# First weights and rows in a written order, first scale spread by TensorE, and the keys of the third dilation laid side by side

## Chip, cores and metric

The kernel runs on one core of a Trainium2 chip. The metric is the time of one execution in device microseconds, as the median of several runs. The engines are TensorE (PE; its weight loads are shown as PEld), VectorE (DVE), ScalarE (ACT), GpSimd (POOL) and SyncE (SP), which here only issues transfers.

## What is computed

One layer of a decoder block on x of 2048 rows and 1024 columns, in float32, cut to what matters here:

```python
h = rmsnorm(x, norm_pre_mix)
proj = h @ w_in                                  # 1024 x 5376
q, k = rope(proj[..., Q0:K0]), rope(proj[..., K0:V0])   # 12 heads of 64
v = proj[..., V0:U0]
# three groups of four heads: dilation 1, 4, 16; each residue class is a causal
# band over 128-query blocks
y_attn = softmax-merge of the three groups
y_gmlp = gelu(u) * spatial(layernorm(gelu(z)))
x = x + rmsnorm((gate_a * (y_attn @ w_a) + gate_b * (y_gmlp @ w_b)) @ w_out, norm_post_mix)
x = x + rmsnorm(relu(rmsnorm(x, norm_pre_mlp) @ w_mlp_in) ** 2 @ w_mlp_out, norm_post_mlp)
```

With dilation 16 a sequence of 2048 has 16 residue classes of 128 positions each, so one block of queries sees one block of keys.

## The kernel before

Rows go in four chunks `c` of 512, each of four blocks `i` of 128. Matrix products run as three matmuls (`mm3`, lines 95 to 97): every operand is split into a rounded high half (fp32r) and the rest, the low half, and high times high, high times low and low times high are added up in PSUM. `split` (lines 70 to 78) makes the halves: a copy for the high one on ScalarE or POOL, a subtraction for the low one on VectorE or POOL.

The program is written in a framework that places the semaphores. TensorE's instructions run in the order in which they are written (line 56). On the other engines and on SP's queue a scheduler orders them by the place in the text and by what is ready in its own model of the times, except where a block is put under `as_written()` (the order of the text on ScalarE, VectorE, POOL and SP) or under `behind()` (each instruction is queued behind the last one so far on its engine, with no wait for its end). Before the change both are used only in the MLP, from line 1143 on.

The start: the scale `norm_pre_mix` is broadcast to 128 partitions by a transfer of 512 KB on ScalarE's queue (`gpre`, line 330). Six fp32 matmuls on a tile of ones (`busy`, line 339) run while the first rows come. The loads of the first rows, of the identity and of the three first weights (`raws`, each in two halves, g = 0, 1, 2) are queued on SP. `prenorm_rows` squares the rows of a block, makes the reciprocal root (`rstd_of`) and multiplies rows, rstd and scale on VectorE (line 192). `prenorm_cols` transposes the block on TensorE (line 202), splits the transposes into `hT` (lines 205 and 206) and, for the first two chunks, copies them once more and stores them (lines 209 and 210). `v_block` then projects a block to the values: for block (0,0) group 0, group 1, the transposes of block (0,1), group 2; for the later ones both wide groups in one, with the transposes of the next block after half of the steps. The split of the first weights is dealt out to POOL, ScalarE and VectorE by `early_split`.

Then `qk_pair` makes queries and keys (`which` 0 and 1) of the three dilations. VectorE multiplies by cosine and sine into `t1` and `t2`, POOL adds or subtracts into `r` with the columns in the order of the dilation (lines 287, 289, 293), ScalarE and VectorE split `r`, and the result is stored in `qk_d`.

Attention runs in 48 units of one dilation `g`, one chunk or residue class `c`, one head `j`, four blocks `b` each, with projection steps (`steps`) between its parts on TensorE. `attn_load` brings `kp` and `qq`; for g = 2 `kp` holds the queries and `qq` the keys. The scores of the third dilation are the four matmuls at line 580, with `kp` as the stationary and `qq` as the moving side; those of the others are at lines 583 and 584. Line 580's operands are `kp[:, b:512:4]` and `qq[:, :, b::4]`: in the stored order the four residues of a class group lie next to each other, and a block takes every fourth element. After the units `combine` merges the three dilations; its transposes are at line 689.

Of the kernel before, what the change touches and what calls it, by code (L numbers as in the profile page):

```python
# [27 lines left out]
def f32(ap):  # L28
    return ap.bitcast(F32) if ap.dtype != F32 else ap
# [12 lines left out]
def block_kernel(ctx, tc, a, out):  # L42
# [120 lines left out]
    sm = stack(e1, "sm", 2)  # L163
    st = stack(e1, "st", 2)

    hT = {}
    xts = {}

# [8 lines left out]
            sp.dma_start(xt[:, sl], x[c * 512 + i * P:c * 512 + (i + 1) * P, sl])  # L177
        xts[c, i] = xt

    def prenorm_rows(c, i):  # L180

        if (c, i) not in xts:
            load_x(c, i)
        xt = xts[c, i]
        ss = sm.tile([P, 2], F32, name=f"ss_{c}{i}", tag="ss")
        for hf in range(2):
            junk = psum_aux(f"junk_{c}{i}{hf}")
            act.activation(junk, xt[:, hf * 512:(hf + 1) * 512], AF.Square, accum_out=ss[:, hf:hf + 1])
        dve.tensor_add(ss[:, 0:1], ss[:, 0:1], ss[:, 1:2])
        r = rstd_of(sm, ss[:, 0:1], 1, 1.0 / D, f"pre{c}{i}")  # L190
        for sl in cuts(c, i):
            dve.scalar_tensor_tensor(xt[:, sl], xt[:, sl], r, gpre[:, sl], op0=OP.mult, op1=OP.mult)

    def prenorm_cols(c, i):

        if i == 0:
            hT[c] = hp.tile([P, 2, KT, 512], F32R, name=f"hT_a{c}", tag="hT", bufs=2)
        h, xt = hT[c], xts.pop((c, i))
        for k in range(0, KT, 4):
            pt = psum_aux(f"pt_{c}{i}{k}")  # L200
            for kk in range(4):
                pe.transpose(pt[:, kk * P:(kk + 1) * P], xt[:, (k + kk) * P:(k + kk + 1) * P], ident)
            hh, hl = (h[:, o, k:k + 4, i * P:(i + 1) * P] for o in range(2))
            p3 = pt.rearrange("p (k t) -> p k t", k=4)
            act.activation(hh, p3, AF.Copy)
            dve.tensor_sub(hl, p3, f32(hh))
            if c < 2:
                raw = xp.tile([P, 4, P], F32, name=f"hr_{c}{i}{k}", tag="hr", bufs=3)
                act.activation(raw, p3, AF.Copy)
                sp.dma_start(hT_d[c, :, k:k + 4, i * P:(i + 1) * P], raw)  # L210
# [55 lines left out]
    def qk_pair(rp, w, g, which, c, rope, between=None):  # L266
        d = DIL[g]
        dst = qk_d[g][which]
        nm = f"{g}{which}{c}"
        pp = []  # L270
        for m in range(2):
            p = psum_mm(f"x{m}_{nm}")
            for n, _ in enumerate(steps_T(w, m, c, p)):
                if between and n in (3, 7):
                    between(m * 2 + n // 4)
            pp.append(p)
        p1, p2 = pp
        cs, sn = rope[:, 0, :], rope[:, 1, :]
        hl = rp.tile([P, 4, 512], F32R, name=f"hl_{nm}", tag="hl", bufs=2)
        for o, (pa, pb, op) in enumerate(((p1, p2, OP.subtract), (p2, p1, OP.add))):  # L280
            t1 = rp.tile([P, 512], F32, name=f"t1_{nm}{o}", tag="t1", bufs=2)
            t2 = rp.tile([P, 512], F32, name=f"t2_{nm}{o}", tag="t2", bufs=2)
            dve.tensor_mul(t1, pa, cs)
            dve.tensor_mul(t2, pb, sn)
            r = rp.tile([P, 512], F32, name=f"r_{nm}{o}", tag="r", bufs=2)
            if d == 1:
                pool.tensor_tensor(r, t1, t2, op=op)  # L287
            elif d == 4:
                pool.tensor_tensor(r.rearrange("p (r l) -> p r l", r=d),
                                   t1.rearrange("p (l r) -> p r l", r=d),  # L290
                                   t2.rearrange("p (l r) -> p r l", r=d), op=op)
            else:
                pool.tensor_tensor(r.rearrange("p (m l r) -> p m l r", m=4, r=4),
                                   t1.rearrange("p (l m r) -> p m l r", m=4, r=4),
                                   t2.rearrange("p (l m r) -> p m l r", m=4, r=4), op=op)
# [31 lines left out]
    with ExitStack() as e1a:  # L327
        xp = stack(e1a, "xp", 2)
        gpre = xp.tile([P, D], F32, name="gpre", bufs=1)
        act.dma_start(gpre, bcast(a["norm_pre_mix"]))  # L330
        act.activation(warm, eps, AF.Sqrt)
        rp = stack(e1a, "rp", 1, side="right")

        busy = rp.tile([P, 256], F32, name="busy", tag="t1", bufs=2)
        dve.memset(busy, 1.0)
        for n in range(2):
            p = psum_aux(f"busy{n}")
            for _ in range(3):
                pe.matmul(p[:, :256], busy[:, :P], busy, start=True, stop=True)
        load_x(0, 0)  # L340
        sp.dma_start(ident, a["ident"])
        raws = [rp.tile([P, 2, 4, 256], F32, name=f"raw{g}", tag=t, bufs=2) for g, t in enumerate(("hl", "hl", "vt"))]
        wide0 = wide_tiles("wv0")
        third0 = wp.tile([P, 2, 2, 4, 256], F32R, name="wv02", tag="w", bufs=3)
# [3 lines left out]
            for kk in range(2):  # L348
                sp.dma_start(raws[g][:, kk], w_src(6 + g, kk))

        def early_split(g, *engs):
            for kk in range(2):
                w = part(wide0[kk], g) if g < 2 else third0[:, kk]
                split(w[:, 0], w[:, 1], raws[g][:, kk], *engs[kk])

        early_load(0)
        load_x(0, 1)
        early_load(1)
        early_load(2)
        prenorm_rows(0, 0)  # L360
        early_split(0, ("pool", "dve"), ("act", "dve"))
        prenorm_cols(0, 0)
        prenorm_rows(0, 1)
        early_split(1, ("act", "pool"), ("act", "dve"))
        early_split(2, ("act", "dve"), ("pool", "dve"))
        blocks = [(c, i) for c in range(4) for i in range(4)]
        qk = [(g, which) for g in range(3) for which in range(2)]
        for half in range(2):
            ropes = {}
            for c in (2 * half, 2 * half + 1):  # L370
                ropes[c] = rp.tile([P, 2, 512], F32, name=f"rope{c}", tag="rope", bufs=2)
# [12 lines left out]
            for n, (g, which) in enumerate(qk):  # L384
                w = nxt
                if n + 1 < len(qk):
                    g2, w2 = qk[n + 1]
                    nxt = load_w(w2 * 3 + g2, f"wq{g2}{w2}{half}")
                elif not half:
                    wv = load_wide(6, "wv1"), load_w(8, "wv12")  # L390
                qk_pair(rp, w, g, which, 2 * half, ropes[2 * half])
                between = None
                if not half and n == 5:
                    for i in range(4):
                        prenorm_rows(2, i)
                    between = lambda i: prenorm_cols(2, i)
                qk_pair(rp, w, g, which, 2 * half + 1, ropes[2 * half + 1], between)
# [156 lines left out]
    def attn_unit(g, c, j):  # L554
# [18 lines left out]
        for b2 in range(2):  # L573
            sp_ = psum_aux(f"s_{nm}{b2}")
            for i in range(2):
# [1 line left out]
                w0, bsl = info[b][0], slice(b * P, (b + 1) * P)  # L577
                o = sp_[:, i * 256:(i + 1) * 256]
                if g == 2:
                    pe.matmul(o.rearrange("p (h k) -> p h k", h=2), kp[:, b:512:4], qq[:, :, b::4],  # L580
                              start=True, stop=True)
                else:
                    pe.matmul(o, qq[:, 0, bsl], kp[:, w0:w0 + 256], start=True, stop=False)
                    pe.matmul(o, qq[:, 1, bsl], kp[:, w0:w0 + 256], start=False, stop=True)
# [555 lines left out]
                    lone_a(1, q, n_, raw.rearrange("p (k c) -> p k c", k=4))  # L1140


    def as_written():
        t = mybir.EngineType
        return tc.manual_schedule(engines={t.Activation, t.DVE, t.Pool, t.SP})

    def behind():

        es, t = ExitStack(), mybir.EngineType
        for e in (t.Activation, t.DVE, t.Pool, t.SP):  # L1150
            es.enter_context(tc.issue_after(next(i for i in reversed(nc.cur_bb.bb.instructions) if i.engine == e)))
        return es

    first_half, second_half = 1, 0
    e2.close()
    ea, ew = ExitStack(), ExitStack()
# [548 lines left out]
```

## Time and profile before

| | us |
|---|---|
| median of 3 runs (2775.97, 2776.09, 2780.45) | 2776.09 |
| the profiled execution | 2779.44 |
| its span | 2777.7 |
| mean granted clock of TensorE, share of full | 0.991 |
| busy: PE / DVE / ACT / POOL | 2712.0 / 1545.2 / 1051.9 / 947.3 |

Times in the trace count from the start of the span. A row of a timeline has start, length, engine, line and operation, output<-inputs, shapes and count; in brackets stands how long the engine had been idle before it and what released it. A row with a count over 1 merges that many instructions.

### The profile page before, as it was taken

What the parts mean: (1) busy time and instruction counts of PE and PEld (TensorE: products, weight loads), DVE (VectorE), ACT (ScalarE), POOL (GpSimd) and SP (SyncE); (2) the same over time, 40 slices, a digit from 0 to 9 for tenths busy, and PEclk for the clock granted to TensorE, in tenths of its full rate; (3) what the DMA queues carried; (4) which work ended last, traced back from release to release, by engine and by line L of the source; (5) the groups of instructions that cost most, each with busy time, mean ns of one, the idle gap of its engine ahead of it and who ended that gap; (6) DMA issues with size and microseconds to landing.
All of it is one profiled execution on the core that took longest, in us unless ns stands there. A gap on an engine that the chain in (4) does not pass through costs nothing. (4 is left out here: it accounts for less than half of the span.)

```text
span 2777.7 us, 34732 instructions
## 1 busy us (share of the span) xinstructions
PE 2712.0 (98%) x12668; PEld 2242.3 (81%) x12668; DVE 1545.2 (56%) x2643; ACT 1051.9 (38%) x2151; POOL 947.3 (34%) x777
## 2 busy tenths in 40 slices
PE   9999999999999999999999999999999999999998
PEld 7888888888878887787787788878887887777787
DVE  5655552344453344554556644555436777777766
ACT  5213111244453321354444544555444333233334
POOL 0341341200000013312215432223314766677645
PEclk9999999999999999999999999999999999999999
DMA  7445455466666654655658534554343122222236
GB/s 266 168 145 169 156 152 195 126 190 195 193 217 192 190 166 149 186 190 160 183 171 268 168 103 125 181 168 126 106 146 108 54 84 84 84 84 84 84 106 213
DMA packets 298380, 426.00 MB, mean 153 GB/s; under 512 B 18528, under 2 KB 172384, under 8 KB 298208
## 3 DMA queue, kind: packets, MB, share of 16 engines
q1 hardware_dynamic: 210368, 372.12, 42.3%
q10 hardware_dynamic: 87840, 51.65, 6.2%
q8 instruction: 100, 1.64, 0.2%
q14 instruction: 72, 0.59, 0.1%
HBM read 282.99 MB, written 140.71 MB: 153 GB/s over the span
## 5 line engine op out<-in xcount | busy, mean ns | idle before, releaser
L1556 PE MATMUL ya<-T_spots,s 128*128 128x512 f32 x1272 | 313.1, 392 | 4.8 <-DVE acc L1564 2.7
L1556 PEld LDWEIGHTS ya<-T_spots,s 128*128 128x128 f32 x1272 | 239.0, 188 | 59.0 <-issue 4.5
L70 ACT ACTIVATE s<-sraw 128x768 fp32r<-128x768 f32 (+1 forms) x184 | 126.0, 695 | 358.2 <-POOL sraw L1355 199.0
L1016 PE MATMUL aa<-B,A 128*128 128x512 f32 x768 | 187.0, 396 | 6.3 <-ACT xs L1030 5.1
L78 DVE TENSOR_TENSOR s<-sraw,s 128x512 fp32r<-128x512 f32 x171 | 163.6, 979 | 34.6 <-ACT s L70 33.0
L987 POOL TENSOR_TENSOR s<-w1r 128x512 f32<-128x512 f32 x32 | 43.5, 1359 | 397.3 <-DVE S L78 337.3
L1016 PEld LDWEIGHTS aa<-B,A 128*128 128x128 f32 x768 | 145.5, 190 | 40.5 <-ACT xs L1030 6.0
L72 POOL TENSOR_SCALAR w_g<-w_g_r 128x1024 fp32r<-128x1024 f32 x32 | 34.1, 1082 | 412.3 <-PE g L97 313.7
L1556 PE MATMUL yc<-T_spots,s 128*128 128x512 f32 x624 | 164.1, 394 | 3.6 <-POOL T_spots L78 3.6
L95 PE MATMUL x<-hT_a,wq 128*128 128x512 f32 x384 | 149.7, 390 | 0.0
L97 PE MATMUL x<-hT_a,wq 128*128 128x512 f32 x384 | 149.4, 389 | 0.0
L96 PE MATMUL x<-hT_a,wq 128*128 128x512 f32 x384 | 149.4, 389 | 0.0
L1556 PEld LDWEIGHTS yc<-T_spots,s 128*128 128x128 f32 x624 | 115.8, 188 | 33.6 <-POOL T_spots L78 9.7
L653 DVE TENSOR_REDUCE o<-po 128x256 f32<-128x512 f32 x48 | 33.1, 690 | 187.5 <-PE po L652 187.5
L78 POOL TENSOR_TENSOR T_spots<-w2r,T_spots 128x512 fp32r<-128x512 f32 x86 | 123.2, 1459 | 5.4 <-ACT T_spots L70 5.4
L70 ACT ACTIVATE hl<-r 128x512 fp32r<-128x512 f32 x48 | 30.4, 633 | 233.2 <-POOL r L287 89.0
L95 PE MATMUL g<-hT_b,w_g 128*128 128x512 f32 x256 | 105.0, 410 | 0.0
L95 PE MATMUL g<-hT_a,w_g 128*128 128x512 f32 x256 | 104.8, 409 | 0.0
L95 PE MATMUL o<-wo,mg 128*128 128x512 f32 x256 | 100.8, 394 | 4.1 <-ACT mg L70 4.1
L70 ACT ACTIVATE S<-w1r 128x512 fp32r<-128x512 f32 x96 | 60.0, 629 | 112.0 <-PE ac L1016 66.6
L815 POOL TENSOR_TENSOR g<-g,g 128x512 f32<-128x512 f32 x28 | 38.8, 1385 | 185.9 <-DVE g L813 179.2
L1354 POOL TENSOR_TENSOR sraw<-sraw 128x256 f32<-128x256 f32 x56 | 41.3, 737 | 174.6 <-DVE s L78 160.3
(379 smaller groups left out, 7214.4 us busy)
## 6 DMA issues: line engine op xcount, KB each, us to landing
w1r<-in_w_mlp_in_dram SPq DMA_DIRECT2D x64, 512.0 KB, 3.6
sraw<-sd SPq DMA_DIRECT2D x128, 256.0 KB, 3.4
qk<-hl SPq DMA_DIRECT2D x24, 1024.0 KB, 5.4
qq<-qk SPq DMA_DIRECT2D x96, 256.0 KB, 5.1
w_g_r<-in_w_in_dram SPq DMA_DIRECT2D x32, 512.0 KB, 5.3
gated<-gt SPq DMA_DIRECT2D x64, 256.0 KB, 3.4
g<-gated SPq DMA_DIRECT2D x64, 256.0 KB, 4.4
w2r<-in_w_mlp_out_dram SPq DMA_DIRECT2D x16, 1024.0 KB, 6.0
```

The costliest lines, as they stand in the source:

```text
L70: act.activation(hi, src, AF.Copy)
L72: pool.tensor_scalar(hi, src, 1.0, 1.0, op0=OP.mult, op1=OP.mult)
L78: (pool if lo_eng == "pool" else dve).tensor_sub(lo, src, f32(hi))
L95: pe.matmul(ps, lh, rh, start=start, stop=False)
L96: pe.matmul(ps, lh, rl, start=False, stop=False)
L97: pe.matmul(ps, ll, rh, start=False, stop=stop)
L653: dve.tensor_reduce(ot[:, :, j * 64:(j + 1) * 64], po.rearrange("p (b h e) -> p b e h", b=4, h=2), axis=AX.X, op=OP.add)
L815: (dve if dt == KT - 1 else pool).tensor_add(parts[0], parts[0], parts[1])
L987: pool.tensor_add(s1, a21, a22)
L1016: pe.matmul(p, w[:, l, k, :], h[:, r, k, :], start=i in (1, 6, 5) and not k and not n, stop=k == 3 and n == 2, skip_group_check=True)
L1354: pool.tensor_add(a22, a21, a22)
L1556: pe.matmul(p, s[:, l], w[:, r], start=i in (1, 2, 5) and not m and not o, stop=m == 1 and o == 2, skip_group_check=True)
```

## The change

1. The scale is loaded as one row of 4 KB into a zeroed tile and spread to all partitions by two fp32 matmuls with a tile of ones (`gp`, in PSUM). The first rows are multiplied from there; ScalarE copies `gp` to `gpre` later, for the rows that follow. The identity is loaded on ScalarE's queue instead of SP's.
2. Five filling matmuls stand ahead of the spread, and two behind it.
3. The loads, the preparation of block (0,0) and of the rows of (0,1), and the split of the first weights stand in a block under `as_written()`, with the shares of the engines dealt out anew. The copies and stores of the transposes of (0,0) (`keep_cols`) go to its end. What is traced from there to the end of `v_block` of (0,1) is queued `behind()` it; that includes the load of the rows of (0,2).
4. In the third dilation the keys (not the queries) are written with the rows of one residue side by side in runs of 32, by POOL's addition, and line 580 reads its moving side in these runs.

`as_written` and `behind` only move up in the text. The diff, with that move left out:

```diff
-    def prenorm_rows(c, i):
+    def prenorm_rows(c, i, gs=None):
...
-        for sl in cuts(c, i):
-            dve.scalar_tensor_tensor(xt[:, sl], xt[:, sl], r, gpre[:, sl], op0=OP.mult, op1=OP.mult)
+        for n, sl in enumerate(cuts(c, i)):
+            dve.scalar_tensor_tensor(xt[:, sl], xt[:, sl], r, gs[n] if gs else gpre[:, sl], op0=OP.mult, op1=OP.mult)
...
     def prenorm_cols(c, i):
...
+        kept = []
         for k in range(0, KT, 4):
...
             dve.tensor_sub(hl, p3, f32(hh))
+            kept.append((k, p3))
+            if (c, i) != (0, 0):
+                keep_cols(c, i, kept)
+        return kept
+
+    def keep_cols(c, i, kept):
+        while kept:
+            k, p3 = kept.pop(0)
             if c < 2:
                 raw = xp.tile([P, 4, P], F32, name=f"hr_{c}{i}{k}", tag="hr", bufs=3)
                 act.activation(raw, p3, AF.Copy)
...
-                pool.tensor_tensor(r.rearrange("p (m l r) -> p m l r", m=4, r=4),
-                                   t1.rearrange("p (l m r) -> p m l r", m=4, r=4),
-                                   t2.rearrange("p (l m r) -> p m l r", m=4, r=4), op=op)
+                order = "l r" if not which else "r l"
+                pool.tensor_tensor(r.rearrange(f"p (m {order}) -> p m {order}", m=4, r=4),
+                                   t1.rearrange(f"p (l m r) -> p m {order}", m=4, r=4),
+                                   t2.rearrange(f"p (l m r) -> p m {order}", m=4, r=4), op=op)
...
-        act.dma_start(gpre, bcast(a["norm_pre_mix"]))
+        rp = stack(e1a, "rp", 1, side="right")
+
+        row = rp.tile([P, D], F32, name="row", tag="rope", bufs=2)
+        busy = rp.tile([P, 256], F32, name="busy", tag="t1", bufs=2)
+        pool.memset(row, 0.0)
+        dve.memset(busy, 1.0)
         act.activation(warm, eps, AF.Sqrt)
-        rp = stack(e1a, "rp", 1, side="right")
-
-        busy = rp.tile([P, 256], F32, name="busy", tag="t1", bufs=2)
-        dve.memset(busy, 1.0)
+        act.dma_start(row[0:1], a["norm_pre_mix"])
+        act.dma_start(ident, a["ident"])
+        p = psum_aux("busy")
+        for _ in range(5):
+            pe.matmul(p[:, :256], busy[:, :P], busy, start=True, stop=True)
+        gp = [psum_mm(f"gpre{n}") for n in range(2)]
         for n in range(2):
-            p = psum_aux(f"busy{n}")
-            for _ in range(3):
-                pe.matmul(p[:, :256], busy[:, :P], busy, start=True, stop=True)
+            pe.matmul(gp[n], busy[:, :P], row[:, n * 512:(n + 1) * 512], start=True, stop=True)
         load_x(0, 0)
-        sp.dma_start(ident, a["ident"])
...
-        def early_split(g, *engs):
-            for kk in range(2):
-                w = part(wide0[kk], g) if g < 2 else third0[:, kk]
-                split(w[:, 0], w[:, 1], raws[g][:, kk], *engs[kk])
-
-        early_load(0)
-        load_x(0, 1)
-        early_load(1)
-        early_load(2)
-        prenorm_rows(0, 0)
-        early_split(0, ("pool", "dve"), ("act", "dve"))
-        prenorm_cols(0, 0)
-        prenorm_rows(0, 1)
-        early_split(1, ("act", "pool"), ("act", "dve"))
-        early_split(2, ("act", "dve"), ("pool", "dve"))
+        def early(g, kk):
+            w = part(wide0[kk], g) if g < 2 else third0[:, kk]
+            return w[:, 0], w[:, 1], raws[g][:, kk]
+
+        def hi(g, kk):
+            w = early(g, kk)
+            act.activation(w[0], w[2], AF.Copy)
+
+        def lo(g, kk, eng):
+            w = early(g, kk)
+            eng.tensor_sub(w[1], w[2], f32(w[0]))
+
+        with as_written():
+            early_load(0)
+            load_x(0, 1)
+            early_load(1)
+            early_load(2)
+            prenorm_rows(0, 0, gp)
+            p = psum_aux("busy")
+            for _ in range(2):
+                pe.matmul(p[:, :256], busy[:, :P], busy, start=True, stop=True)
+            hi(0, 0)
+            hi(0, 1)
+            lo(0, 0, dve)
+            kept = prenorm_cols(0, 0)
+            lo(0, 1, dve)
+            hi(1, 0)
+            hi(1, 1)
+            lo(1, 0, pool)
+            lo(1, 1, dve)
+            for n in range(2):
+                act.activation(gpre[:, n * 512:(n + 1) * 512], gp[n], AF.Copy)
+            prenorm_rows(0, 1)
+            hi(2, 0)
+            hi(2, 1)
+            lo(2, 1, pool)
+            lo(2, 0, dve)
+            keep_cols(0, 0, kept)
+        first = behind()
...
                 v_block(rp, wv, c, i, between)
+                if (c, i) == (0, 1):
+                    first.close()
...
-                    pe.matmul(o.rearrange("p (h k) -> p h k", h=2), kp[:, b:512:4], qq[:, :, b::4],
-                              start=True, stop=True)
+                    pe.matmul(o.rearrange("p (h c l) -> p h c l", h=2, c=4),
+                              kp[:, b:512:4],
+                              qq.rearrange("p h (c r l) -> p r h c l", c=4, r=4)[:, b], start=True, stop=True)
```

More of the change, by code (lines that the diff above doesn't have):

```diff
@@ L164, in block_kernel, with as_written, behind @@
     st = stack(e1, "st", 2)
+    def as_written():
+        t = mybir.EngineType
+        return tc.manual_schedule(engines={t.Activation, t.DVE, t.Pool, t.SP})
+    def behind():
+        es, t = ExitStack(), mybir.EngineType
+        for e in (t.Activation, t.DVE, t.Pool, t.SP):
+            es.enter_context(tc.issue_after(next(i for i in reversed(nc.cur_bb.bb.instructions) if i.engine == e)))
+        return es
     hT = {}
@@ L1140, in block_kernel @@
                     lone_a(1, q, n_, raw.rearrange("p (k c) -> p k c", k=4))
[L1143 to L1152, printed above, removed]
     first_half, second_half = 1, 0
```

## The prediction

> **What bounds the kernel now.** I read the page first, then the table of windows, then the timelines of the first 30 us engine by engine, then one unit of the third dilation.
>
> ```profile
> span 2777.7 us, 34732 instructions
> PE 2712.0 (98%) x12668; PEld 2242.3 (81%) x12668; DVE 1545.2 (56%) x2643; ACT 1051.9 (38%) x2151; POOL 947.3 (34%) x777
> 0.00:12.28 12.28, 7.36 (x21) 5.47 (x21) 4.80 (x13) 4.88 (x9) 1.45 (x6) 0.92 0.81 273
> 22.80:40.00 17.20, 17.20 (x111) 15.26 (x110) 9.73 (x24) 10.08 (x26) 0.00 (x0) 1.00 0.81 284
> ...
> 850.00:1003.00 153.00, 152.93 (x800) 131.77 (x800) 56.03 (x206) 57.38 (x188) 10.33 (x10) 1.00 0.55 171
> ```
>
> The columns of a window are its length, busy time of PE, PEld, DVE, ACT and POOL, granted clock, DMA share and GB/s. TensorE is busy 98% of the span. In the stage of the third dilation (850 to 1003) it has no gap at the full clock, so a microsecond taken from it there comes off the end. Only the start is not set by it (7.36 busy of the first 12.28 us, most of that filling matmuls, and a stall until 21.17 shown below): loads, ScalarE and VectorE set it. From 22.8 on it does not stop, so what counts of the start is how much earlier that unbroken stream runs. The change touches these two places.
>
> **The start now.**
>
> ```profile
> 1.31 5.49 PE L339 MATMUL busy<-busy 128*128 128x256 f32 x12 [1.31 <-DVE busy L335]
> 10.41 1.94 PE L202 MATMUL pt<-ident,x 128*128 128x128 f32 x8 [3.61 <-DVE x L192]
> 21.17 0.39 PE L96 MATMUL va<-wv,hT_a 128*128 128x256 f32 x1 [1.35 <-DVE wv L78]
> 29.23 1.06 PE L202 MATMUL pt<-ident,x 128*128 128x128 f32 x8
> 1.24 1.28 ACT L331 ACT_TABLE_LOAD   x1 [1.24 <-PEq L1693]
> 6.70 0.60 ACT L188 ACTIVATE junk<-x 128x512 f32<-128x512 f32 x1 [0.20 <-DMA x<-in_x_dram]
> 9.92 1.06 ACT L70 ACTIVATE wv<-raw 128x1024 fp32r<-128x1024 f32 x1 [1.98 <-DMA raw<-in_w_in_dram]
> 15.06 1.07 ACT L209 ACTIVATE hr<-pt 128x512 f32<-128x512 f32 x2
> 16.19 2.01 ACT L70 ACTIVATE wv<-raw 128x1024 fp32r<-128x1024 f32 x2
> 8.81 2.16 DVE L192 SCALAR_TENSOR_TENSOR x<-x,r_pre,gpre 128x512 f32<-128x512 f32 x2
> 15.23 2.40 POOL L78 TENSOR_TENSOR wv<-raw,wv 128x1024 fp32r<-128x1024 f32 x1 [5.46 <-ACT wv L70]
> 16.66 7.32 SPq L177 DMA_DIRECT2D x<-in_x_dram  x4
> raw<-in_w_in_dram SPq DMA_DIRECT2D x6, 512.0 KB, 8.8
> gpre<-in_norm_pre_mix_dram ACTq DMA_DIRECT2D x1, 512.0 KB, 5.2
> ```
>
> The first columns are start and length. The second half of the first rows lands at 6.70 (ScalarE waits for it), the second weight half at 9.92. VectorE writes the scaled rows from 8.81 to 10.97, TensorE transposes from 10.41, and its projection stream stalls until 21.17. The last transposes of interest, those of row block (0,2), begin at 29.23 and TensorE does not wait for them. That is my marker: how much earlier they begin in the new kernel is the gain of the start.
>
> **Terms of the start.**
> (1) The broadcast of the scale, 512 KB, is replaced by one row of 4 KB, and the identity goes to ScalarE's queue. At the 273 GB/s of the first window 512 KB are 1.9 us of transfer. The raws are queued on SP behind the rows, so they should land up to 1.9 us sooner, and at the least not later: I take 1.8 (the transfers are near their full share, 0.81). The second weight half then lands at 8.1, the rows at about 5.
> (2) The spread: one matmul of 256 fp32 columns is two records, twelve take 5.49 us, so 0.45 each at the cold clock. Five matmuls end at 1.31 + 10 x 0.43 = 5.6. The two of 512 columns are four records of twice the length, 3.4 us cold, 1.7 warm: gp is there between 7.5 and 9.0. That is later than rstd could be (it follows the rows by about 2.1 us, 6.70 to 8.81, so 7.1), but its cover is ScalarE, which holds the first two weight halves until 8.1 + 1.06 = 9.2 before it copies a transpose. The multiply by gp is 2.16 us for two halves now, beside a POOL operation; alone half of the shape 128x1024 (1.28), some 0.7 each. Transposes run about 9 to 10. The two further matmuls (0.9 to 1.8 us) stand ahead of them on TensorE and fill the time in which it waits for VectorE.
> (3) The clock.
>
> ```profile
> 10.00:11.00 1.00, 0.59 (x3) 0.62 (x4) 0.97 (x2) 0.98 (x1) 0.00 (x0) 0.63 0.97 356
> ...
> 17.00:18.00 1.00, 1.00 (x10) 1.00 (x10) 0.93 (x3) 1.00 (x2) 1.00 (x2) 0.96 1.05 293
> ```
>
> It is halved from shortly after 10.2, after 3.6 us in which TensorE was idle, and comes back at 17.1. With TensorE kept going this stretch should go. But the stall until 21.17 is VectorE's, so the clock alone is worth nothing at the marker; it lets the shorter chains show. [...]
> (4) ScalarE's written order sets the rest. From 8.1: one weight half 1.06, two copies of transposes 1.07, two weight halves 2.01 (12.3), two copies of gp at 1.07 (13.3), two squares and reads of the next rows 1.35 (24.22 to 25.57 in the rows below; 14.7), the sum and the root (0.6 of the 1.3 that lie between the end of the reads and the multiply, 7.5 to 8.81), two weight halves 2.01 (17.3), two copies for the store 1.07. Now those copies start at 15.06 and the load of (0,2) is issued at 16.66 behind their two stores, 1.6 later. The new order ties this load to the last store of the written block, so it is issued at 17.3 + 1.6 = 18.9, that is 2.2 us later than now.
>
> ```profile
> 24.22 0.62 ACT L188 ACTIVATE junk<-x 128x512 f32<-128x512 f32 x1
> 25.36 0.21 ACT L188 ACTIVATION_READ_ACCUMULATOR junk<-x 128x1 f32 x1
> 27.80 1.28 DVE L192 SCALAR_TENSOR_TENSOR x<-x,r_pre,gpre 128x1024 f32<-128x1024 f32 x1
> x<-in_x_dram SPq DMA_DIRECT2D x9, 512.0 KB, 3.7
> ```
>
> It lands some 3.5 us later (22.4; 3.7 is the median above); squares 1.35, rstd 1.3, the multiply 1.28 and 0.15 (29.08 to 29.23) bring the transposes of (0,2) to 26.5: 29.23 - 26.5 = **2.7 us**. TensorE alone would be there sooner. POOL's low half (2.40 after a weight half that ends at 11.3) frees the second group at 13.7; 24 matmuls at 0.12 (846.26 to 846.38 below) end at 16.6; the next rows' transposes at 17.5 to 18.4; the third group waits for its low half until about 19.3 (an estimate: VectorE starts it at 17.3, beside POOL's other half) and ends at 22.1; half of block (0,1) takes 2.8. That is 24.9, so TensorE now waits some 1.6 us for the load. Behind this new wait on SP stand the loads of later rows and weights; no engine waits for them before 40 in either order. Bounds of the start: 4.3 (TensorE alone decides) and 0 (the raws land no sooner than now: the chain then ends at 28.3, and a slip in the steps that VectorE and POOL do side by side takes the rest).
>
> **Third dilation.**
>
> ```profile
> 854.98 0.31 PEld L580 LDWEIGHTS s<-qq,kp 128*128 128x128 f32 x1
> 855.19 0.81 PEld L580 LDWEIGHTS s<-qq,kp 128*128 128x128 f32 x3
> 855.40 0.89 PE L580 MATMUL s<-qq,kp 128*128 128x256 f32 x3
> 855.90 0.21 PEld L95 LDWEIGHTS g<-hT_b,w_g 128*128 128x128 f32 x1
> 856.12 0.41 PE L95 MATMUL g<-hT_b,w_g 128*128 128x512 f32 x1
> 846.26 0.28 PE L583 MATMUL s<-kp,qq 128*128 128x256 f32 x1
> 846.38 0.28 PE L584 MATMUL s<-kp,qq 128*128 128x256 f32 x1
> L580 PEld LDWEIGHTS s<-qq,kp x64: 308/334/337, 855.0 to 991.5; 128*128 128x128 f32 x64
> L583 PEld LDWEIGHTS s<-kp,qq x128: 187/188/337, 539.4 to 846.4; 128*128 128x128 f32 x128
> ```
>
> A unit has four score matmuls, and there are 16 units (64 records). Every fourth element is read, on both sides. Three of them lie between 855.40 and 856.12: 0.24 each, where the same 256 columns of neighbours side by side take 0.12 (846.26 to 846.38). The fourth is followed by a weight load of neighbours (855.90) and still takes 0.24, so the moving read is slow by itself. The change lays the keys, the moving side, side by side in runs of 32; the queries, the stationary side, keep their step. Their load takes 0.334 against 0.188; the first, with no such matmul beside it, lets the next begin after 0.21. So a unit, now 856.12 - 854.98 = 1.14, becomes 4 x 0.21 + 0.12 = 0.96: 16 x 0.18 = **2.9 us**. Bounds: if the load hides behind the matmul, 0.21 + 4 x 0.12 = 0.69, 7.2 us; if it alone sets the pace, 0. I take 2.9 because 0.12 x 334/188 is 0.21 as well. [...]
>
> POOL's part of the key change:
>
> ```profile
> L289 POOL TENSOR_TENSOR r<-t,t x16: 2137/2199/2578, 145.8 to 387.4; 128x512 f32<-128x512 f32 x16
> L293 POOL TENSOR_TENSOR r<-t,t x16: 1262/1268/2240, 189.3 to 430.0; 128x512 f32<-128x512 f32 x16
> 200.00:437.00 237.00, 237.00 (x1169) 200.65 (x1168) 127.33 (x171) 43.69 (x85) 78.69 (x56) 1.00 0.48 155
> ```
>
> Eight of the sixteen at L293 (the keys') now gather with a wide step, as L289 does: 8 x 0.93 = 7.4 us more on an engine that is busy 79 of 237 us, while TensorE has no gap. L289's cost hides there already, so I put this at nothing; uncovered it would be at most 7.4 us. Bytes stored and loaded stay the same.
>
> **Sum.** The profiled execution took 2779.44 (span 2777.7 and 1.7 around it); 2.7 + 2.9 = 5.6 gives 2773.8. The median of the three runs, 2776.09, is 3.35 lower, so I forecast 2776.09 - 5.6 = 2770.5. The 0.2% that a measurement can tell from no change are 5.55 us, so the forecast stands on that line.
>
> **Rivals.**
> - The stationary load hides: 7.2 + 2.7, 2766.2. For it: weight loads overlap matmuls everywhere. Against it: the 0.21 of the first load. Chance 0.15.
> - The load of (0,2) is not what ends last and TensorE decides: 4.3 + 2.9, 2768.9. For it: raws may land sooner than 1.8. Chance 0.15.
> - The start brings 0.7 or less since the raws still land late: 2772.5. For it: raws take 8.8 us now and their bytes are the same. Chance 0.12.
> - [...] Chance 0.06.
> - The 4 KB row comes late: slower. It may be issued only after ScalarE's table load (1.24 + 1.28 and a short activation, 2.8) and shares the transfer engines with 4.1 MB that are queued on SP; TensorE, in written order, holds everything behind gp. Up to a landing at 6 (gp at 9.4) nothing is lost, from there each us costs one, and at 11.6 the gain of both parts is gone. Behind all first loads, 4.1 MB at 273 GB/s, it lands at about 15: the start loses 9 - 2.7 = 6.3, the clock drops again (3.4 us at half speed, 1.7), and the kernel takes 2776.09 + 6.3 + 1.7 - 2.9 = 2781.2. Against it: gpre, 128 times the bytes, landed in 5.2. Chance 0.07.
>
> ```profile
> PE yt L689 <- POOL A L684: 5.1, 1, 5.1
> ```
>
> - The scheduler orders the engines anew outside the written blocks, and this wait before the merge doubles: 2770.5 + 5.1, 2775.6. Nothing in the trace asks for it. Chance 0.05.
>
> **How the numbers follow.** The forecast has 0.40, half of it past the 0.2%. Faster by over 0.2%: 0.20 + 0.15 + 0.15, and 0.04 where the cases of 2772.5 and 2773.4 meet a hidden load, 0.54. Slower by over 0.2%: 0.04, the half of the late row with the latest landings, and 0.03 where more than one wait of the last case grows, 0.07. The rest, 0.39, lies within. The range reaches from 2765.5, under the first rival, to 2776.5, over the last; outside lie the late row and the tails.
>
> **What would show it.** Right: no halved clock before 40; gp's matmuls done by 9; the transposes of (0,2) at 26 to 27 after a wait for VectorE of 1 to 2 us; L580's matmuls 0.21 apart with loads still at 0.33 and the last one followed after 0.12; POOL's key operations at 2.2 with no gap of TensorE beside them. Wrong: L580 still at 0.24, or at 0.12; (0,2) at 29 or later; a gap of TensorE ahead of gp that ends on a DMA.

## The result and the profile after

| | before | after |
|---|---|---|
| median of 22 runs each, us | 2779.88 (2775.97 to 2782.01) | 2775.24 (2770.39 to 2777.99) |
| ratio, with its 95% interval | | 0.9985 (0.9979 to 0.9990) |
| the profiled execution, us | 2779.44 | 2772.85 |
| its span, us | 2777.7 | 2771.1 |
| mean granted clock | 0.991 | 0.993 |

The new kernel is faster by 0.15%, about 4.2 us, where 5.6 were forecast. The interval lies below 1 but reaches from 0.10% to 0.21%, so the sign is measured; the median doesn't cross the 0.2% line, and the interval just reaches over it. Two of the three runs of before that stood in the prediction were the lowest of all 22 of their kernel (median 2776.09 against 2779.88). The forecast of 2770.5 was counted from them; from 2779.88 the same sum gives 2774.3, which is one microsecond under what was measured. That nearness is no proof of the steps: the forecast had 2.7 us from the start and 2.9 from the third dilation, and the trace has neither.

First the page and the windows of the profile after, in the columns of before:

```profile
span 2771.1 us, 34747 instructions
PE 2706.7 (98%) x12674; PEld 2237.1 (81%) x12674; DVE 1547.4 (56%) x2642; ACT 1055.8 (38%) x2155; POOL 951.9 (34%) x777
0.00:12.28 12.28, 9.68 (x38) 7.29 (x39) 6.05 (x15) 7.27 (x12) 1.30 (x6) 1.00 0.81 288
12.28:22.80 10.52, 7.06 (x54) 6.28 (x53) 9.25 (x12) 8.24 (x17) 5.00 (x2) 0.99 0.79 290
22.80:40.00 17.20, 16.90 (x97) 15.01 (x97) 8.09 (x21) 8.21 (x23) 0.00 (x0) 0.91 0.84 282
...
850.00:1003.00 153.00, 152.83 (x809) 131.61 (x808) 54.44 (x206) 57.13 (x185) 10.32 (x10) 1.00 0.53 169
```

The clock now stays at 1.00 in the first window (0.92 before), and is lost in the third instead (0.91, where before had 1.00). For the very first microseconds the column doesn't tell the pace: it reads 1.00 there too, while the ten records of the filling take 4.51 us, 0.45 each, where the same record takes 0.24 later (eight in 1.89, under filled below). In the middle window TensorE is busy for only 7.06 of 10.52 us. Something there stops it, and the timelines of TensorE, ScalarE, VectorE and POOL say what:

```profile
1.31 4.51 PE L362 MATMUL busy<-busy 128*128 128x256 f32 x10 [1.31 <-DVE busy L356]
5.66 1.88 PE L365 MATMUL gpre<-row,busy 128*128 128x512 f32 x4
8.24 1.04 PE L214 MATMUL pt<-ident,x 128*128 128x128 f32 x8
18.79 1.06 PE L214 MATMUL pt<-ident,x 128*128 128x128 f32 x8 [0.71 <-DVE x L203]
22.01 0.39 PE L96 MATMUL vb<-wv,hT_a 128*128 128x256 f32 x1 [2.04 <-DVE wv L386]
25.33 0.41 PE L95 MATMUL vb<-wv,hT_a 128*128 128x256 f32 x1
25.54 0.41 PE L96 MATMUL vb<-wv,hT_a 128*128 128x256 f32 x1
26.37 0.40 PE L95 MATMUL va<-wv,hT_a 128*128 128x512 f32 x1
29.59 0.63 PE L214 MATMUL pt<-ident,x 128*128 128x128 f32 x4 [0.30 <-DVE x L203]
8.75 1.06 ACT L382 ACTIVATE wv<-raw 128x1024 fp32r<-128x1024 f32 x1 [0.24 <-DMA raw<-in_w_in_dram]
26.57 0.39 ACT L343 ACTIVATE vt<-vb 128x256 fp32r<-128x256 f32 x1 [1.68 <-PE vb L97]
26.86 0.29 ACT L102 ACTIVATE r_pre<-ss,edge 128x1 f32<-128x1 f32 x1
11.53 1.21 DVE L386 TENSOR_TENSOR wv<-raw,wv 128x1024 fp32r<-128x1024 f32 x1
17.36 1.29 DVE L203 SCALAR_TENSOR_TENSOR x<-x,r_pre,gpre 128x1024 f32<-128x1024 f32 x1
18.56 3.40 DVE L386 TENSOR_TENSOR wv<-raw,wv 128x1024 fp32r<-128x1024 f32 x1
28.16 1.28 DVE L203 SCALAR_TENSOR_TENSOR x<-x,r_pre,gpre 128x1024 f32<-128x1024 f32 x1
18.47 2.41 POOL L386 TENSOR_TENSOR wv<-raw,wv 128x1024 fp32r<-128x1024 f32 x1 [3.45 <-ACT wv L382]
7.44 2.19 SPq L188 DMA_DIRECT2D x<-in_x_dram  x3
18.89 0.94 SPq L230 DMA_DIRECT2D hTd<-hr  x2
```

The same places in the timeline of TensorE before (the transposes of the rows of (0,1), the second matmul of the third group behind them, the first matmul behind that group):

```profile
22.58 1.03 PE L202 MATMUL pt<-ident,x 128*128 128x128 f32 x8
23.57 0.28 PE L96 MATMUL vb<-wv,hT_a 128*128 128x256 f32 x1
26.32 0.40 PE L95 MATMUL va<-wv,hT_a 128*128 128x512 f32 x1
```

Read down, the rows are the story of a lead that is won and lost. The second weight half is in ScalarE's hands at 8.75 instead of 9.92. The spread takes its four records in 1.88 us, and the first transposes stand at 8.24 instead of 10.41. Those of (0,1) stand at 18.79 instead of 22.58: by then the new start leads by 3.79 us.

Then the third weight's low halves are made by VectorE and POOL at the same moment (18.56 and 18.47), and VectorE's takes 3.40 us where the same subtraction took 1.21 at 11.53. TensorE waits 2.04 us for it, and at the second matmul of the third group (22.01 against 23.57) the lead is 1.56. (Before's own stall, the one until 21.17, lies one group earlier, ahead of the transposes of (0,1).) Behind the stall the matmuls of the group lie 0.21 apart (25.33, 25.54), at half clock, and at the first matmul behind the group (26.37 against 26.32) nothing is left of the lead. ScalarE's copy of the group's result (26.57) stands in its queue ahead of the root for the rows of (0,2) (26.86), so these wait for TensorE too; their transposes begin at 29.59, after 0.30 of waiting. Before had 29.23. The start is 0.36 us **later**, and TensorE's place in its stream stays some 0.35 us behind before until about 770 us.

Where the 3.40 us come from is hinted at by the ends. VectorE's subtraction ends at 21.96 and POOL's at 20.88, 1.08 apart. The pair that is made for the second weight starts otherwise, VectorE 1.25 us behind POOL (13.67 and 12.42), and ends the same way, at 16.10 and 15.02. In both pairs of broadcast and the later one of no_fill the distance is 1.08 us as well. So VectorE's looks as if it stood until POOL's was done and then took 1.08 us, little less than the 1.21 at 11.53. This is an estimate from these rows. low_dve, below, takes POOL's half away and shows that the delay comes with it, but not how.

In the third dilation the timeline of TensorE around the first unit, its weight loads, and the line's groups read:

```profile
853.95 1.19 PE L631 MATMUL s<-qq,kp 128*128 128x256 f32 x4
854.98 0.39 PE L95 MATMUL g<-hT_b,w_g 128*128 128x512 f32 x1
853.92 1.02 PEld L631 LDWEIGHTS s<-qq,kp 128*128 128x128 f32 x4
854.84 0.21 PEld L95 LDWEIGHTS g<-hT_b,w_g 128*128 128x128 f32 x1
L631 PEld LDWEIGHTS s<-qq,kp x64: 308/330/338, 853.9 to 989.0; 128*128 128x128 f32 x64
L631 PE MATMUL s<-qq,kp x64: 395/399/485, 853.9 to 989.1; 128*128 128x256 f32 x64
```

From the first load of a unit (853.92) to the next matmul of a projection (854.98) it is 1.06 us, against 1.14. The loads still last 0.33. The next load of neighbours starts at 854.84, so the four take 0.92 together, 0.23 each. Before has the same 0.92 (854.98 to 855.90): the pace of the loads is unchanged, and only the last matmul got shorter. Sixteen units by 0.08 make 1.3 us, and TensorE's lead over before goes from 1.05 (at 786) to 2.40 us (at 973).

So the traces show a start that lost 0.35 and a third dilation that won some 1.3. The rest of the gap between these two profiled executions, 6.6 us, lies where both kernels do the same work: in the stretches at half clock (before has 6.83 us of it from 771.43 to 778.26, after 3.41 from 773.57 to 776.98) and in waits near 1160 to 1180 and behind 1500. At 1150 to 1190 all nine other traces gain on this one of before, by 0.4 to 3.2 us, and the one with the old start and new keys (keys_only below) does too; so part of it belongs to this one execution of before. The executions of one kernel differ by as much (2770.39 to 2777.99), so those pieces are not read as an effect of the change.

### The profile page after: what moved, and what is told of

Its sections match the earlier page's. It is cut to its first block, busy times and chain, and to the rows that moved or that the text cites. A ratio compares the mean times of both kernels' runs of the same rounds, so it can differ in the third digit from the quotient of the medians.

```text
span 2771.1 us, 34747 instructions
## 1 busy us (share of the span) xinstructions
PE 2706.7 (98%) x12674; PEld 2237.1 (81%) x12674; DVE 1547.4 (56%) x2642; ACT 1055.8 (38%) x2155; POOL 951.9 (34%) x777
```

## The experiments

Two questions were put. For the third dilation: does the stationary side's step set the pace (the theory after the trace), or does it hide once the moving side is contiguous and the trace only looks so? For the start: was the lead lost to the two low halves made side by side and the half clock behind them (the theory), or to a late landing of the rows of (0,2) or of the row of the scale, as the prediction and its rivals had it? All ratios are to the kernel before on the same chip.

**keys_only**: the kernel before with part 4 alone.

```diff
-                pool.tensor_tensor(r.rearrange("p (m l r) -> p m l r", m=4, r=4),
...
+                order = "l r" if not which else "r l"
+                pool.tensor_tensor(r.rearrange(f"p (m {order}) -> p m {order}", m=4, r=4),
...
-                    pe.matmul(o.rearrange("p (h k) -> p h k", h=2), kp[:, b:512:4], qq[:, :, b::4],
-                              start=True, stop=True)
+                    pe.matmul(o.rearrange("p (h c l) -> p h c l", h=2, c=4),
+                              kp[:, b:512:4],
+                              qq.rearrange("p h (c r l) -> p r h c l", c=4, r=4)[:, b], start=True, stop=True)
```

> The kernel before with the key layout alone. Theory K (the stationary load, still stepping by four, sets the pace of the scores, and only the last matmul of a unit gets shorter): a unit's four scores take 1.06 instead of 1.14 us, so 16 x 0.08 = 1.3 us less, the stage reached at the same time as before, about -0.05% and not to be told from no change by the total. Rival (the layout brings the whole measured gain): about -4 us, -0.15%, with the scores at 0.12 to 0.2 apart.

Measured: 0.9997 (0.9989 to 1.0006), median 2779.37. The loads last 308 to 330 ns and the score matmuls 395 to 398, as in after. Alone, the part is worth less than these runs can tell from nothing; 1.3 us are 0.05% and fit.

**start_only**: the kernel after with the keys in the old order and the old line 580.

```diff
-                order = "l r" if not which else "r l"
-                pool.tensor_tensor(r.rearrange(f"p (m {order}) -> p m {order}", m=4, r=4),
...
+                pool.tensor_tensor(r.rearrange("p (m l r) -> p m l r", m=4, r=4),
...
-                    pe.matmul(o.rearrange("p (h c l) -> p h c l", h=2, c=4),
-                              kp[:, b:512:4],
-                              qq.rearrange("p h (c r l) -> p r h c l", c=4, r=4)[:, b], start=True, stop=True)
+                    pe.matmul(o.rearrange("p (h k) -> p h k", h=2), kp[:, b:512:4], qq[:, :, b::4],
+                              start=True, stop=True)
```

> The changed kernel with the old key layout. Theory L (the third group's low half, 3.40 us on VectorE beside POOL's, gives the start's lead back): the projection again stalls about 2.0 us ahead of the third group, the transposes of block (0,2) begin between 28.0 (clock kept) and 29.6 (clock halved), and the total is 0 to 1.5 us less than before, plus what the clock does. Rival (the start brings the measured gain): about -3 us, -0.11%, and the transposes of (0,2) at 27 or earlier.

Measured: 0.9994 (0.9985 to 1.0002), median 2778.48. The timeline of TensorE has the same stall:

```profile
22.31 0.58 PE L96 MATMUL vb<-wv,hT_a 128*128 128x256 f32 x1 [2.04 <-DVE wv L385]
29.75 0.52 PE L214 MATMUL pt<-ident,x 128*128 128x128 f32 x3 [0.30 <-DVE x L203]
```

The marker is 0.52 us behind that of before, just outside the expected 28.0 to 29.6. The start of the new kernel wins nothing in either of the two traces, this one and after. The two halves add to 0.09%; the whole measures 0.15%. The intervals overlap, so this isn't a contradiction, but some 1.7 us of the measured gain have no place in these two runs.

**both_sides**: the kernel after, with the queries stored in runs of 32 by residue as well, so that the stationary side is contiguous too.

```diff
-                order = "l r" if not which else "r l"
+                order = "r l"
...
+            if d == 16 and not which:
+                dd = bass.AP(tensor=dst.tensor, offset=dst.offset + c * 32, ap=[[4 * S, P], [128, 64], [1, 32]])
+                sp.dma_start(dd, f32(hl).rearrange("p o (m l) -> p (o m) l", l=32))
...
-                              kp[:, b:512:4],
+                              kp[:, b * P:(b + 1) * P],
```

> The changed kernel with the queries of the third dilation, too, side by side by residue (stored in runs of 32 columns), so that the stationary side reads neighbours. Theory K: weight loads fall from 0.33 to 0.19 us, scores stand 0.12 apart, a unit takes about 0.6 instead of 1.06, 16 x 0.46 = 7.4 us less than the changed kernel, about 2768. Rival (the scores wait for something else, such as the step between PSUM or the issue): 0.2 or more apart still, no gain. A cost may come from the store in pieces of 128 bytes: a gap of TensorE between 180 and 440 us would show it.

Measured: 0.9964 (0.9951 to 0.9978), median 2770.06. The line's groups and the first unit:

```profile
L635 PEld LDWEIGHTS s<-qq,kp x64: 187/189/193, 855.9 to 984.5; 128*128 128x128 f32 x64
855.89 0.54 PEld L635 LDWEIGHTS s<-qq,kp 128*128 128x128 f32 x4
856.36 0.19 PEld L95 LDWEIGHTS g<-hT_b,w_g 128*128 128x128 f32 x1
856.48 0.39 PE L95 MATMUL g<-hT_b,w_g 128*128 128x512 f32 x1
```

Four loads now end in 0.47 us (855.89 to 856.36), 0.12 each, half of the 0.23 with the step. The unit goes from 1.06 to 0.59. Sixteen times 0.47 are 7.5 us; the median is 5.2 us below that of after, and the interval has room for either. That settles what held after: with the step on the stationary side the load sets the pace, 0.23, though the moving side is contiguous. The third combination, contiguous queries with keys in steps, was not run. In before the last matmul of a unit, with its keys in steps and a load of neighbours behind it, still takes 0.22 to 0.24, so little is to be expected of it. The store in pieces of 32 cost TensorE no wait between 100 and 540 us.

**low_dve**: the kernel after with both of the third weight's low halves on VectorE, one after the other.

```diff
-            lo(2, 1, pool)
             lo(2, 0, dve)
+            lo(2, 1, dve)
```

> The changed kernel with both low halves of the third group on VectorE, one after the other, and POOL idle meanwhile. Theory L: each takes 1.2 us, the projection's stall ahead of the third group falls from 2.0 to about 0.2 us, no halved clock before 40, and the transposes of (0,2) begin at about 27.6, where they wait for their rows: 1.5 to 2 us less than the changed kernel. Rival (the rows of (0,2), loaded behind the written block, end last in any case): the transposes stay at 29 to 29.6.

Measured: 0.9971 (0.9960 to 0.9983), median 2773.02. The timelines of VectorE and TensorE:

```profile
19.01 2.35 DVE L386 TENSOR_TENSOR wv<-raw,wv 128x1024 fp32r<-128x1024 f32 x2
20.06 0.36 PE L95 MATMUL vb<-wv,hT_a 128*128 128x256 f32 x1
20.28 0.39 PE L96 MATMUL vb<-wv,hT_a 128*128 128x256 f32 x1
26.57 1.06 PE L214 MATMUL pt<-ident,x 128*128 128x128 f32 x8 [0.53 <-DVE x L203]
```

One engine makes both halves in 2.35 us; with POOL beside it VectorE's half alone took 3.40. The 2.04 us stall is gone, the granted clock reads 1.00 from 0 to 40 us, and the marker is at 26.57, 2.66 us ahead of before and a microsecond sooner than expected (27.6). It meets the 26.5 of the prediction by number only: there the load of (0,2) was to end last; here TensorE waits 0.53 us for the multiply of the rows, and SP issues that load at 7.93. The late landing of (0,2) is refuted with it: nothing in this kernel makes that load earlier than in after (7.44), and its rows are multiplied by 26.43.

**filled**: the kernel after with four filling matmuls behind the last transposes of (0,1), in the place of the stall.

```diff
+            f = psum_aux("fill")
+            for _ in range(4):
+                pe.matmul(f[:, :256], busy[:, :P], busy, start=True, stop=True)
```

> The changed kernel with four more filling fp32 matmuls of 256 columns (1.7 us at the full clock) on TensorE between the transposes of block (0,1) and the third group, inside the stall of 2.0 us. Theory C (of what the start gives back, the clock that is halved after that stall is a part of its own): no halved clock before 40, the third group at 0.12 per matmul, the transposes of (0,2) at about 27.8 instead of 29.6, and the total about 1.5 us under the changed kernel. Rival (the stall on VectorE alone decides): the third group starts at 22.0 as before and the transposes stay within 0.5 us of 29.6.

Measured: 0.9983 (0.9974 to 0.9992), median 2774.90.

```profile
19.25 1.89 PE L335 MATMUL fill<-busy 128*128 128x256 f32 x8
21.58 0.38 PE L96 MATMUL vb<-wv,hT_a 128*128 128x256 f32 x1 [0.33 <-DVE wv L389]
27.28 1.06 PE L214 MATMUL pt<-ident,x 128*128 128x128 f32 x8
18.12 3.41 DVE L389 TENSOR_TENSOR wv<-raw,wv 128x1024 fp32r<-128x1024 f32 x1
```

VectorE's subtraction is as slow as in after (3.41), and TensorE gets past it hardly sooner: 1.89 us of filling and 0.33 of waiting stand where the stall was. But the clock is kept, and the marker comes at 27.28, 2.31 us ahead of after. Of these, 0.43 is an earlier end of the stall (21.58 against 22.01), which is not the filling's doing: in this execution the second weight half landed 0.45 sooner (8.30 against 8.75). The matmuls of the group that follow, 4.36 us in after (22.01 to 26.37), take 2.86 here (21.58 to 24.44), and the wait of 0.30 ahead of the marker is gone. So about 1.5 us of the lost lead were the half clock. The ratio can't be told from that of after: the medians differ by 0.3 us where 1.5 were expected. The trace shows the difference.

**no_fill**, one execution: the kernel after without its seven filling matmuls.

```diff
-        p = psum_aux("busy")
-        for _ in range(5):
-            pe.matmul(p[:, :256], busy[:, :P], busy, start=True, stop=True)
...
-            p = psum_aux("busy")
-            for _ in range(2):
-                pe.matmul(p[:, :256], busy[:, :P], busy, start=True, stop=True)
```

> The changed kernel without its seven filling matmuls. Theory L (VectorE's low half sets the third group): the clock is halved through the first group, which ends up to 3 us later, but the third group still starts at 22 to 22.5 and the transposes of (0,2) within 1 us of 29.6, for the second group and VectorE's steps do not wait for the first. Rival (keeping TensorE going is what the start's lead comes from): the whole start is 2 to 3 us later, the transposes at 31.5 or later.

One time, 2779.61, beside a median of 2779.69 of before. The timeline of TensorE:

```profile
4.53 3.39 PE L362 MATMUL gpre<-row,busy 128*128 128x512 f32 x4 [4.53 <-DMA row<-in_norm_pre_mix_dram]
21.95 0.58 PE L96 MATMUL vb<-wv,hT_a 128*128 128x256 f32 x1 [2.04 <-DVE wv L383]
30.28 0.96 PE L214 MATMUL pt<-ident,x 128*128 128x128 f32 x7
```

The spread starts when the row lands, at 4.53, and takes 3.39 us on a TensorE that has not run yet, against 1.88. It ends at 7.92 instead of 7.54: at that place the filling bought 0.4 us. The half clock that was expected through the first group did not come: the granted clock is 1.00 from 8 to 20. The stall is the same 2.04. The stretch at half clock is 6.8 us long (21.08 to 27.91), and the marker 0.69 later than in after. The run also shows when the row was there: about 2.7 us after its issue at 1.78, with 1.1 us to spare ahead of the 5.66 at which after uses it. That the marker would be at 30.28 in every run is more than one execution can say.

**broadcast**, one execution: the kernel after with the scale broadcast by the old transfer of 512 KB, and nine filling matmuls in place of five and the spread.

```diff
-        act.dma_start(row[0:1], a["norm_pre_mix"])
+        act.dma_start(gpre, bcast(a["norm_pre_mix"]))
...
-        for _ in range(5):
+        for _ in range(9):
...
```

> The changed kernel with the scale broadcast by a transfer of 512 KB on ScalarE's queue as before, no spread by TensorE, and four more filling matmuls in its place; written order unchanged. Theory (the spread is worth the transfer time of 512 KB): the second first weight half lands 1.2 to 1.9 us later than the changed kernel's 8.75, the third group starts at about 23.5 and the transposes of (0,2) begin at 30.5 to 31.2. Rival (the raws land when they did): the landing stays within 0.5 us of 8.75 and the marker at 29.6.

One time, 2776.05. The timelines of ScalarE and TensorE:

```profile
5.39 0.60 ACT L199 ACTIVATE junk<-x 128x512 f32<-128x512 f32 x1 [2.64 <-DMA x<-in_x_dram]
9.80 1.06 ACT L377 ACTIVATE wv<-raw 128x1024 fp32r<-128x1024 f32 x1 [0.19 <-DMA raw<-in_w_in_dram]
23.15 0.38 PE L96 MATMUL vb<-wv,hT_a 128*128 128x256 f32 x1 [2.03 <-DVE wv L381]
```

With the 512 KB back, the second weight half lands at 9.80, where the seven traces with the row have it between 8.15 (no_fill) and 9.19 (low_dve), 8.60 in the middle; the two with the old start have 9.92 and 9.93. Against the middle one the smaller transfer is worth 1.2 us there, against after 1.05, a little under the forecast. The stall ends 1.14 later (23.15), but in this run the clock stayed up behind it (1.00 in the windows from 16 to 28), having been lost from 11.94 to 15.36 instead, and the marker came at 29.22 where 30.5 to 31.2 were expected. So in this pair of executions the half clock of after eats what the spread wins.

A stall of 2.03 us (21.12 to 23.15) kept the clock here, and one of 2.04 (19.97 to 22.01) lost it in after. The half-clock stretch of after lasts 3.41 us (22.64 to 26.05), and that of broadcast about as long. Why the one stall lost the clock and the other did not, no run shows, so the clock behind such a stall can't be forecast from its length.

**all_best**: both_sides and low_dve together (their two diffs).

> The changed kernel with both low halves of the third group on VectorE and with both sides of the third dilation side by side. If the two act in different places, their gains add up: marker at 26.6, a score every 0.12 us, 2.5 plus 6 to 7.5 us under the changed kernel, about 2766, ratio to before 0.994 to 0.995. If a later wait (the merge, the stage from 1150 on) gives part of it back, less: 0.996.

Measured: 0.9949 (0.9936 to 0.9963), median 2766.23 (2763.70 to 2767.26), against 2779.69 before. The marker in the timeline of TensorE:

```profile
26.18 1.06 PE L214 MATMUL pt<-ident,x 128*128 128x128 f32 x8 [0.53 <-DVE x L203]
```

The two remedies add up: 0.36% and 0.29%, less the 0.15% that both contain, make 0.50%, and 0.51% were measured. This version beats both kernels.

## Why the prediction was right and wrong

**The sign and the size.** A small gain about the 0.2% line was forecast and 0.15% measured. That the sum came out near is luck: its terms were 2.7 and 2.9, the trace has -0.35 and 1.3, the base was 3.8 us below the median of 22 runs, and most of what was measured has no place among the terms.

**Term (1), the raws.** Forecast 1.8 us sooner, measured 1.17 (9.92 to 8.75), and 0.6 to 1.65 over the traces against the 9.80 of broadcast. The mechanism is right; the size, taken as all of the 512 KB at the window's rate, was at the upper end.

**Term (2), the spread.** gp was to be there between 7.5 and 9.0 and is there at 7.54. The row came in time: in no_fill, where nothing stands ahead of the spread, it is used at 4.53, and 6 was the point from which the rival of the late row would cost. TensorE's first transposes begin at 8.24, sooner than the 9 to 10 that were forecast.

**Term (3), the clock.** The step failed. The forecast was that the half clock of the start goes away and that it is worth nothing at the marker. In after it did go from 10.2 to 17.1 (the granted clock is 1.00 from 10 to 22; in start_only and broadcast about 3.4 us of it stayed, from about 12 to 15.3), but a new one came from 22.64 to 26.05, behind the stall. There it counts: ScalarE's copy of the group's result, and behind it the root for the next rows, wait for TensorE. filled prices it at 1.5 us. The stretch lasts 3.41 us, half of before's 6.82 (10.26 to 17.08). Before has one of that length too, from 1174.20 to 1177.61; it is the 3.4 us at half speed in the sum for the late row. How much idle time loses the clock these rows don't settle: 2.04 us of it lost the clock in after, and 2.03 did not in broadcast.

**Term (4), the chain to (0,2).** The step failed in both of its parts. The load of (0,2) is not tied to the last store: SP issues it at 7.44, the stores from 18.89. The account of the kernel ahead of the prediction is wrong there. On SP's queue the last instruction that `behind()` finds is the entry that closes the written block, not the last store, so SP is not held. And the low half, called ready at about 19.3, was ready at 21.96. Of the 2.66 us, 1.26 are its late start (VectorE's multiply of the rows of (0,1), 17.36 to 18.65, stands first) and 1.40 its length, 3.40 where 2.0 had been assumed: it ended 1.08 us behind POOL's. Before had a hint of it that I passed over. Beside POOL's work (2.40 from 15.23, so to 17.63, then a copy to 18.64) two of VectorE's smallest operations are drawn out and end just as POOL's do, at 17.66 and 18.66, in its timeline:

```profile
16.54 1.12 DVE L108 SCALAR_TENSOR_TENSOR t_pre<-r_pre,v_pre 128x1 f32<-128x1 f32 x1
17.88 0.78 DVE L113 TENSOR_TENSOR r_pre<-r_pre,t_pre 128x1 f32<-128x1 f32 x1
19.89 3.49 DVE L78 TENSOR_TENSOR wv<-raw,wv 128x1024 fp32r<-128x1024 f32 x3
```

In after they take 0.22 and 0.16 with POOL idle, and the three low halves of the last row, made by VectorE alone, take 1.16 each. The forecast was that TensorE alone would be done at 24.9; the late half and the clock move that by 2.66 and 1.5 to 29.06; 0.30 of waiting for the rows of (0,2) and some 0.2 of small differences make the 29.59.

**The third dilation.** The mechanism on the moving side is right: the last matmul of a unit is shorter with contiguous keys, 0.14 us against 0.22 to 0.24. The size failed: 0.21 for a stepped load was read from one pair of loads in before (854.98 to 855.19) that had no matmul ahead of it; the second reason, 0.12 x 334/188, gave the same number by chance. The four loads of that unit, 854.98 to 855.90, had the pace of 0.23 already. In after the loads follow each other every 0.23, and both_sides shows 0.12. The forecast's lower bound, a stationary load that alone sets the pace, is the case, with the last matmul as its 1.3 us. The step costs time on the stationary side as well: a load takes 0.330 with it (after) and 0.189 without (both_sides).

**The rivals.** Of the rivals, the small start (0.7 or less) came nearest, but not for its reason: the raws did land sooner, and the lead went to a step behind them. A hidden stationary load is refuted by the 0.23 between the loads of after, a free step on the moving side (the case of 2773.4, chance 0.06) by the last matmul of a unit, which takes 0.14 instead of 0.22 to 0.24.

**Right at nothing.** The sixteen POOL operations of that line, half of them the keys', took 6.4 us more together (28.76 against 22.35), where 7.4 were forecast, and that hid: TensorE has no wait from 100 to 540 us. The wait before the merge did not double (5.9 us against 5.1).

**Open.** The measured 0.15% is more than the start and the third dilation show (about 1 us together). keys_only and start_only add to 0.09% with intervals wide enough to take in both. That stretches at half clock fall otherwise in the later stages is seen in the traces (6.83 us against 3.41 between 771 and 779). The runs on record point the same way: the mean granted clock is 0.9924 over the 22 of after and 0.9913 over 39 of before (those beside the experiments), and 1 less the clock, times the time, makes some 21 and 24 us (an estimate). The start's stretch of 3.41 us in place of 6.82, worth 1.7 us (an estimate) and already counted there, is part of that difference. Why the rest of it comes, and whether the change causes it, is not shown.

## What to carry to other kernels

Before work is dealt out to two engines to save time, read from the trace what the operation takes while the other engine runs its like: here VectorE alone did both halves in 2.35 us, and beside POOL its one half took 3.40. When a matmul's operands are read with a step, look at the pace of the loads and the matmuls apart, and mend the side that sets it, or both: the keys' side by itself gave 1.3 us by the rows, the queries' side on top of it another 7.5. A short stall of TensorE can cost more than its own row in the table of waits: here 2.04 us were followed by a stretch at half clock worth 1.5 more, and in another execution a stall as long was not. And a lead is to be read from the same instructions in both traces, place by place; two stalls that look alike can stand at different ones.

## What the runs showed of the hardware

A subtraction of two fp32 operands of 128 x 1024 on VectorE took 1.21 us alone and 2.43 and 3.40 beside the same operation on POOL (2.60 and 2.41); in these two pairs of after and three of broadcast and no_fill it ended 1.08 us behind POOL's. After's stretch at half clock lasted 3.41 us (22.64 to 26.05), broadcast's about as long (11.94 to 15.36), before's 6.82 (10.26 to 17.08). A stationary operand read with a step of four fp32 took 0.330 us to load and held its successor back to 0.23; contiguous it took 0.189 and 0.12. In one execution (no_fill) a row of 4 KB, issued on ScalarE's queue behind the identity, was in use about 2.7 us after its issue, and leaving out all seven filling matmuls cost 0.4 us at the end of the spread.
